# A scaled matmul with an addend on one core: tile 55 stored by GpSimd's queue in 32 pieces, and a last store of four tiles in place of eight

## The chip, the core and the metric

The kernel runs on one NeuronCore of one Trainium2 chip. The metric is the device time of one execution in microseconds (us), the median of three runs. Five engines work beside each other: TensorE (PE) multiplies, VectorE (DVE), ScalarE (ACT) and GpSimd (POOL) move and combine data, and SyncE (SP) issues transfers. Sixteen DMA queues move the data between HBM and the on-chip memory; the profile calls them the core's 16 DMA engines.

## What is computed

```python
def reference(x, weight, scale, add_value):
    # x: 16 x 512 x 1024, weight: 1024 x 768, add_value: 16 x 512 x 768, all float32; scale 0.1
    return (scale * np.matmul(x, weight) + add_value).astype(np.float32)
```

The 16 x 512 rows are taken as 8192 rows of one matrix.

## The kernel before

**Tiles.** The 8192 rows are 64 tiles of 128 rows. Sixteen neighbouring rows of HBM belong to one partition, so that tiles s to s+n-1 of one group are n consecutive rows in HBM for each partition. A transfer of n tiles is thus 128 runs, one for each partition: 4096 n bytes for `x`, 3072 n bytes for `add_value` and the output. Eight output tiles are 24,576 bytes in a partition, four are 12,288, one is 3,072.

**Buffers.** `xs` has 16 slots for tiles of `x`, `ao` has 32 slots which first hold the weights, then the addend and, after the sum is made in place, the output. `slot(t)` gives a tile's slot.

**Engines.** ACT and POOL cast `x` to bf16 and regroup it into `va` (`mover`, line 147, one half of the 32-partition blocks each). DVE transposes four-tile halves of `va` into `xt` (`turn`, line 162), PE multiplies (line 197), and DVE makes scale times product plus addend for two tiles at a time (`finish`, line 171). Each `finish` adds 2 to the semaphore `made`; its value `MADE` + t + 1 says that tiles up to t are done.

**SP's order.** `sync_engine` walks through the list `STREAM`: `w`, `x` and `a` are loads, `("o", s, n)` is the store of tiles s to s+n-1. SP waits for `made` ahead of each store. The first load of `x` (`FIRST`) stands ahead of the block and the last store (`LAST`, tiles 56 to 63, line 237) behind it. All other work stands in one block, `tc.tile_critical`, at whose exit SP collects a signal from every engine's sequencer, POOL's among them, before the store of line 237 is issued. At the very end SP waits for the last store to have landed (line 268).

**The end of the order.** The last transfers on SP are the loads of the addend for tiles 56 to 63, and the stores of tiles 32 to 47, 48 to 55 and 56 to 63. POOL has nothing to do once its last cast is done.

Of the kernel before, what the change touches and what calls it, by code (L numbers as in the profile page):

```python
# [8 lines left out]
P = 128  # L9
G = 8  # L10
R = 16
# [16 lines left out]
]  # L28
FIRST, LAST = (0, 8), (56, 8)


@with_exitstack
def kernel(
# [8 lines left out]
    nc = tc.nc  # L42
# [7 lines left out]
    _, N = weight.shape  # L50
    T = M // P
# [5 lines left out]
    out_v = out_f.rearrange("(g p t) n -> p g t n", p=P, t=R)  # L57
    w_v = weight.rearrange("(c p r) n -> p c (r n)", p=P, r=2)

    def rows(view, s, n):  # L60
        assert s // R == (s + n - 1) // R
        return view[:, s // R, s % R:s % R + n, :]
# [5 lines left out]
    ao = const.tile([P, A_SLOTS, N], fp32, name="ao")  # L68
# [6 lines left out]
    x_sem = [tc.alloc_semaphore(f"x{i}") for i in range(X_SLOTS // MOVE)]  # L75
    a_sem, a_late = (tc.alloc_semaphore(n) for n in ("a", "a_late"))
    o_sem = [tc.alloc_semaphore(f"o{i}") for i in range(2)]
    by_act, by_pool, pool_go, turned, casts, done, made = (
        tc.alloc_semaphore(name)
        for name in ("by_act", "by_pool", "pool_go", "turned", "casts", "done", "made"))  # L80
    TURNED = MOVE * VA_BUFS
    MADE = TURNED + 2 + MM_BUFS - 2

    def slot(t):
        return (t + G) % A_SLOTS

    def sync_engine(eng):
        loads, stores, known = [], [], {}

        def need(sem, value):  # L90
            if known.get(sem, 0) < value:
                eng.wait_ge(sem, value)
                known[sem] = value

        for op, s, n in STREAM:
            last = s + n - 1
            if op == "w":
                dst = ao[:, s:s + n, :].rearrange("p (c r) n -> p c (r n)", r=2)
                move, sem = eng.dma_start(dst, w_v[:, s // 2:(s + n) // 2, :]), w_sem[s // 4]
            elif op == "x":  # L100
                k = s % X_SLOTS
                if last >= X_SLOTS:
                    moved = 8 * (last + 1 - X_SLOTS) // MOVE
                    need(by_act, moved)
                    need(by_pool, moved)
                move = eng.dma_start(xs[:, k:k + n, :], rows(x_v, s, n))
                sem = x_sem[k // MOVE]
            elif op == "a":
                if loads and s % G == 0:
                    need(a_sem, 16 * len(loads))  # L110
                if slot(s) == 0:
                    need(casts, KJ)
                if s >= A_SLOTS:
                    i = next(j for j, (a, b) in enumerate(stores) if a <= s - A_SLOTS < a + b)
                    need(o_sem[i % 2], 16 * (i // 2 + 1))
                move = eng.dma_start(ao[:, slot(s):slot(s) + n, :], rows(add_v, s, n))
                if s % G:
                    sem = a_late
                else:
                    sem = a_sem  # L120
                    loads.append((s, n))
            else:
                i = len(stores)
                if i > 1:
                    need(o_sem[i % 2], 16 * (i // 2))
                need(made, MADE + last + 1)
                move = eng.dma_start(rows(out_v, s, n), ao[:, slot(s):slot(s) + n, :])
                sem = o_sem[i % 2]
                stores.append((s, n))
            move.then_inc(sem, 16)  # L130
            if op == "x" and n == 2 * MOVE:
                eng.sem_inc(x_sem[k // MOVE + 1], 16)

    def mover(eng, copy, parity, count, go=None):
        if go is None:
            eng.preload_act_table(mybir.ActivationFunctionType.Copy)  # L136
        with eng.Fori(16, 16 * (T // X_SLOTS) + 1, 16) as i:
            for q in range(X_SLOTS // MOVE):
                eng.wait_ge(x_sem[q], i)
                eng.wait_ge(turned, i + (4 * q - 12) if q < 3 else i)  # L140
                if go is not None:
                    eng.sem_inc(go, 1)
                k = MOVE * q
                src = xs[:, k:k + MOVE, :].rearrange("p i (c b k) -> p (i c) b k", b=4, k=64)
                for a in (parity, parity + 2):
                    for b in range(4):
                        copy(va[q % VA_BUFS][32 * b:32 * b + 32, :, a, :],  # L147
                             src[32 * a:32 * a + 32, :, b, :]).then_inc(count, 1)

    def vector_engine(eng):  # L150
        ao_g = ao.rearrange("p (g t) n -> p g t n", t=G)

        def cast_w(s, n):
            eng.wait_ge(w_sem[s // 4], 16)
            eng.tensor_copy(w_bf[:, s:s + n, :], ao[:, s:s + n, :]).then_inc(casts, n)  # L155

        def turn(move, half, moves=None):
            if half == 0:
                eng.wait_ge(by_act, moves)
                eng.wait_ge(by_pool, moves)  # L160
            q = 2 * half * KC
            eng.transpose(  # L162
                xt[:, 2 * half:2 * half + 2, :, :].rearrange("p i c m -> p (i c m)"),
                va[move % VA_BUFS][:, q:q + 2 * KC, :, :].bitcast(fp32).rearrange("p c a k -> p (c a k)"),
            ).then_inc(turned, 2)

        def finish(pair, at, products):
            eng.wait_ge(done, products)  # L168
            a = ao_g[:, at, 2 * pair:2 * pair + 2, :]
            q = 2 * (pair % 2)  # L170
            eng.scalar_tensor_tensor(  # L171
                a, mm[:, q:q + 2, 0:N], float(scale), a,
                op0=mybir.AluOpType.mult, op1=mybir.AluOpType.add).then_inc(made, 2)

        def group(i, at, last):
            eng.wait_ge(a_sem, i)
            for p in range(4):
                if p == 2 and not last:
                    eng.wait_ge(a_late, i)
                finish(p, at, i + (4 * p - 12) if p < 3 else i)  # L180
                if p < 2 or not last:
                    turn(1 if p < 2 else 0, p % 2, i + 8 if p == 2 else i)

        cast_w(0, 4)
        cast_w(4, 4)
        turn(0, 0, 8)
        turn(0, 1)
        with eng.Fori(16, 2 * T, 16) as i:
            group(i, bass.ds((i // 16) % (A_SLOTS // G), 1), False)
        eng.addr_align(HALF_BLOCK, offset=PAST)  # L190
        s = slot(T - G) // G
        group(2 * T, slice(s, s + 1), True)
# [12 lines left out]
    def tensor_engine(eng):  # L205
        eng.sem_inc(x_sem[1], 16)
        eng.sem_inc(turned, TURNED)
        eng.sem_inc(made, MADE)
        eng.sem_inc(a_late, 16 * (T // G - 2))
        eng.wait_ge(casts, KJ)  # L210
        with eng.Fori(TURNED + 2, TURNED + 2 + T, XT_TILES) as i:
            for q in range(XT_TILES):
                if q % 2 == 0:
                    eng.wait_ge(turned, i + q if q else i)
                    eng.wait_ge(made, i + q if q else i)
                for j in range(KJ):
                    x2 = xt[:, q, j // 2, :].bitcast(bf16).rearrange("p (m r) -> p r m", r=2)
                    m = product(eng, mm[:, q, :], x2[:, j % 2, :], w_bf[:, j, :], j)
                if q % 2:
                    m.then_inc(done, 4)  # L220


    s, n = FIRST
# [4 lines left out]
    with tc.tile_critical(no_gpsimd_drain=True):  # L228
        sync_engine(nc.sync)
        mover(nc.scalar, nc.scalar.copy, 0, by_act)  # L230
        nc.scalar.addr_align(HALF_BLOCK, offset=PAST)
        mover(nc.gpsimd, nc.gpsimd.tensor_copy, 1, by_pool, pool_go)
        nc.gpsimd.addr_align(HALF_BLOCK, offset=PAST)
        vector_engine(nc.vector)
        tensor_engine(nc.tensor)
    s, n = LAST
    nc.sync.dma_start(rows(out_v, s, n), ao[:, slot(s):slot(s) + n, :])


# [33 lines left out]
```

## Time and profile before

| what | value |
|---|---|
| median of 3 runs | 209.19 us (209.13 to 209.28) |
| span of the profiled execution | 207.5 us |
| what lies around the span, median less span | 1.7 us |
| PE busy | 168.4 us, 81% of the span |
| DVE, ACT, POOL busy | 97.8, 134.7, 135.4 us |
| moved by DMA | 87.06 MB, of which 25.17 MB are written to HBM |

The page of the profiled execution gives its span, the time from the first to the last instruction, and no time of its own beside it. The numbers of the trace below are times from the start of that span. In the views by windows the last two columns are the busy share of the 16 DMA queues and the rate; both count a packet, whole, in the window in which it starts. A packet is one run of bytes, or the 4 bytes that count up a semaphore when a queue has finished its part of a transfer.

### The profile page before, as it was taken

Reading aid. Unit: us, or ns where it says so; the run is one execution under the profiler, and the core shown is the slowest. Engines: PE = TensorE matmul, PEld = TensorE weight load, DVE = VectorE, ACT = ScalarE, POOL = GpSimd, SP = SyncE. Lnnn points to the kernel's source line nnn. Section 1 sums busy time; section 2 is a strip of 40 time slices with the busy share of each in tenths; the row PEclk is TensorE's granted clock in tenths of the full one; section 3 lists DMA queues with packets and bytes.
Section 4 is the critical chain, followed back from the end, with each engine's and each line's share of the span. In section 5 each row is a group of like instructions: output and inputs, shape, how many; then the busy total and the mean of one; then the engine's idle time right before and its main releaser. Section 6 shows DMA issues by size and latency. Waiting matters only on the chain.

```text
span 207.5 us, 2310 instructions
## 1 busy us (share of the span) xinstructions
PE 168.4 (81%) x1024; PEld 50.3 (24%) x512; DVE 97.8 (47%) x66; ACT 134.7 (65%) x129; POOL 135.4 (65%) x132
## 2 busy tenths in 40 slices
PE   0000099999999999999999999999999999999400
PEld 0000023333332222222233333333333333333100
DVE  0005525537555555555555554755555555553300
ACT  2059970799999796969696079999970999300000
POOL 0049994799999996969696079999990899400000
PEclk9999999999999999999999999999999999999955
DMA  7999999999999999999999999999999999999993
GB/s 291 417 381 469 403 466 404 455 455 404 404 467 442 411 398 486 393 441 407 445 436 423 423 436 455 411 445 412 441 414 422 437 445 455 460 417 388 412 441 171
DMA packets 4147, 87.06 MB, mean 420 GB/s; under 512 B 432, under 2 KB 432, under 8 KB 944
## 3 DMA queue, kind: packets, MB, share of 16 engines
q1 hardware_dynamic: 4144, 87.03, 98.1%
q14 instruction: 3, 0.02, 0.0%
HBM read 61.87 MB, written 25.17 MB: 419 GB/s over the span
## 4 chain that ended last, share of the span: by engine, by line
PE 81%; DMA 6%; ACT 5%; DVE 1%; issue 1%; DVEq 0%; ACTq 0%
PE mm L197 81%; DMA xs<-in_x_dram 6%; ACT va L147 5%; DVE ao L171 1%; DVE xt L162 1%; ACTq L140 0%; DVEq L160 0%; DVEq L168 0%
## 5 line engine op out<-in xcount | busy, mean ns | idle before, releaser
L197 PE MATMUL mm<-w_bf,xt 128*128 128x512 bf16 (+1 forms) x1024 | 168.4, 328 | 26.0 <-DVE xt L162 26.0
L147 POOL CAST va<-xs 32x1024 bf16<-32x1024 f32 x128 | 135.2, 1056 | 43.1 <-DMA xs<-in_x_dram 24.7
L147 ACT CAST va<-xs 32x1024 bf16<-32x1024 f32 x128 | 133.4, 1042 | 42.1 <-DMA xs<-in_x_dram 25.8
L171 DVE SCALAR_TENSOR_TENSOR ao<-mm,ao 128x1536 f32 (+1 forms) x32 | 56.3, 1758 | 76.5 <-PE mm L197 76.5
L195 PEld LDWEIGHTS <-xt 128*128 128x128 bf16 x512 | 50.3, 98 | 143.6 <-issue 117.6
L162 DVE STREAM_TRANSPOSE xt<-va 128x1024 f32<-128x1024 f32 x32 | 39.4, 1234 | 3.8 <-ACT va L147 2.1
L155 DVE CAST w_bf<-ao 128x3072 bf16<-128x3072 f32 x2 | 4.5, 2240 | 18.1 <-DMA ao<-in_weight_dram 18.1
L136 ACT ACT_TABLE_LOAD x1 | 1.3, 1283 | 1.3 <-SPq L228 1.3
L254 POOL MEMSET const-float32-0.0<- 128x1 f32 x1 | 0.1, 98 | 0.2 <-issue 0.2
L254 POOL MEMSET const-bfloat16-1.0<- 128x1 bf16 x1 | 0.1, 100 | 0.0
L254 POOL MEMSET const-float32-1.0<- 128x1 f32 x1 | 0.1, 98 | 0.0
L254 POOL MEMSET const-uint8-127<- 128x1 uint8 x1 | 0.1, 97 | 0.0
## 6 DMA issues: line engine op xcount, KB each, us to landing
xs<-in_x_dram SPq DMA_DIRECT2D x7, 4096.0 KB, 20.9
ao<-in_add_value_dram SPq DMA_DIRECT2D x7, 3072.0 KB, 17.0
out_dram<-ao SPq DMA_DIRECT2D x6, 3072.0 KB, 27.0
out_dram<-ao SPq DMA_DIRECT2D x1, 6144.0 KB, 35.4
xs<-in_x_dram SPq DMA_DIRECT2D x2, 2048.0 KB, 19.1
ao<-in_weight_dram SPq DMA_DIRECT2D x2, 1536.0 KB, 16.8
ao<-in_add_value_dram SPq DMA_DIRECT2D x2, 1536.0 KB, 14.9
```

Source lines behind the costliest of these rows:

```text
L136: eng.preload_act_table(mybir.ActivationFunctionType.Copy)
L147: copy(va[q % VA_BUFS][32 * b:32 * b + 32, :, a, :], src[32 * a:32 * a + 32, :, b, :]).then_inc(count, 1)
L155: eng.tensor_copy(w_bf[:, s:s + n, :], ao[:, s:s + n, :]).then_inc(casts, n)
L162: eng.transpose(xt[:, 2 * half:2 * half + 2, :, :].rearrange("p i c m -> p (i c m)"), va[move % VA_BUFS][:, q:q + 2 * KC, :, :].bitcast(fp ...
L171: eng.scalar_tensor_tensor(a, mm[:, q:q + 2, 0:N], float(scale), a, op0=mybir.AluOpType.mult, op1=mybir.AluOpType.add).then_inc(made, 2)
L195: eng.ldweights(x_j, tile_position=(0, 0))
L197: m = eng.add_instruction(mybir.InstMatmult(start_tensor_calc=(j == 0), stop_tensor_calc=(j == KJ - 1), tile_size=(P, P), tile_position=(0 ...
L254: nc = _bacc.Bacc("TRN2", target_bir_lowering=False, num_devices=1)
```

## The change

- The store of tiles 48 to 55 becomes one of tiles 48 to 54 (`("o", 48, 7)`).
- Tiles 56 to 59 get a store of their own on SP behind it, once they are made, with a semaphore `end_sem` that nobody waits for. The last store has tiles 60 to 63.
- Tile 55 is stored by GpSimd's queue (`aside`), behind its last cast and once tile 55 is made. It is cut into 16 sets of eight partitions, each set four partitions apart (q, q+4, ... q+28). Each set is two transfers: one of the last 32 columns of either half of the row (16 runs of 128 bytes, 2 KB), and one of the other 352 columns of either half (16 runs of 1408 bytes, 22 KB). Together they are 32 transfers, 2 KB and 22 KB in turn. They stand inside the block.
- Behind the last store SP waits, in a second small block, until all 32 have landed (`few_sem`).

```diff
-    ("a", 52, 4), ("x", 60, 4), ("a", 56, 8), ("o", 32, 16), ("o", 48, 8),
+    ("a", 52, 4), ("x", 60, 4), ("a", 56, 8), ("o", 32, 16), ("o", 48, 7),
+    ("o", 56, 4),
 ]
-FIRST, LAST = (0, 8), (56, 8)
+FIRST, LAST = (0, 8), (60, 4)
+ASIDE, FEW, STEP, FILL = 55, 8, 4, 32
...
+    few_sem, end_sem = (tc.alloc_semaphore(name) for name in ("few", "end"))
...
+            elif last == T - LAST[1] - 1:
+                need(made, MADE + last + 1)
+                move = eng.dma_start(rows(out_v, s, n), ao[:, slot(s):slot(s) + n, :])
+                sem = end_sem
...
+    def aside(eng):
+        eng.wait_ge(made, MADE + ASIDE + 1)
+        to = out_v[:, ASIDE // R, ASIDE % R, :].rearrange("p (h n) -> p h n", h=2)
+        at = ao[:, slot(ASIDE), :].rearrange("p (h n) -> p h n", h=2)
+        for p in range(0, P, FEW * STEP):
+            for q in range(p, p + STEP):
+                part = slice(q, q + (FEW - 1) * STEP + 1, STEP)
+                for n in (slice(N // 2 - FILL, N // 2), slice(0, N // 2 - FILL)):
+                    eng.dma_start(to[part, :, n], at[part, :, n]).then_inc(few_sem, 16)
...
         nc.gpsimd.addr_align(HALF_BLOCK, offset=PAST)
+        aside(nc.gpsimd)
...
     s, n = LAST
     nc.sync.dma_start(rows(out_v, s, n), ao[:, slot(s):slot(s) + n, :])
+    with tc.tile_critical(no_gpsimd_drain=True):
+        nc.sync.wait_ge(few_sem, 16 * 2 * P // FEW)
```

No other engine's instructions change; the loads, casts, transposes and products keep their order.

## The prediction

> **What bounds the kernel now.** I read the page's slices first, then the DMA queues, the chain, and the end of the run by windows.
>
> ```profile
> PE   0000099999999999999999999999999999999400
> DMA  7999999999999999999999999999999999999993
> q1 hardware_dynamic: 4144, 87.03, 98.1%
> PE 81%; DMA 6%; ACT 5%; DVE 1%; issue 1%; DVEq 0%; ACTq 0%
> ```
>
> Two things are full at once. PE works without a gap from the sixth slice on, and the chain puts 81% of the span on it; but the chain view stops at the last instruction on an engine and leaves out the transfer behind it. The DMA queues are busy for 98.1% of the span. PE sets when the last tiles are made; the queues set when everything has landed.
>
> ```profile
> 26.01 168.37 PE mm L197 x1024
> 194.48 1.76 DVE L171 SCALAR_TENSOR_TENSOR ao<-mm,ao 128x1536 f32<-128x1536 f32 x1 [3.44 <-PE mm L197]
> 196.53 0.33 SPq L237 DMA_DIRECT2D out_dram<-ao  x1
> DMA to landing us min/median/max: 10.1/10.1/10.1
> SPq L268 <- DMA out_dram<-ao: 9.7, 1, 9.7
> ```
>
> The last tile is made at 194.48 + 1.76 = 196.24, the last store is issued at 196.53 and has landed 10.1 us later, at 206.6; SP waits 9.7 us for it. Behind that lie 0.9 us to the span's end at 207.5 and 1.7 us more to the median of 209.19. So the change can act on the 10.1 us alone, or on the time at which they begin.
>
> What fills them is seen in windows (the last two columns are the queues' share and GB/s, by the packets that start in each):
>
> ```profile
> 178.75:196.50 17.75, 15.62 (x97) 4.59 (x47) 9.33 (x6) 0.00 (x0) 0.00 (x0) 1.00 0.99 425
> 196.90:197.30 0.40, 0.00 (x0) 0.00 (x0) 0.00 (x0) 0.00 (x0) 0.00 (x0) 0.53 0.29 123
> 197.35:198.25 0.90, 0.00 (x0) 0.00 (x0) 0.00 (x0) 0.00 (x0) 0.00 (x0) 0.50 1.02 437
> 203.70:204.35 0.65, 0.00 (x0) 0.00 (x0) 0.00 (x0) 0.00 (x0) 0.00 (x0) 0.50 1.41 605
> 204.35:205.15 0.80, 0.00 (x0) 0.00 (x0) 0.00 (x0) 0.00 (x0) 0.00 (x0) 0.50 0.01 0
> 205.20:206.20 1.00, 0.00 (x0) 0.00 (x0) 0.00 (x0) 0.00 (x0) 0.00 (x0) 0.50 0.06 25
> ```
>
> (1) When the last store is issued the queues still hold older stores: 0.99 up to 196.50. (2) From 196.90 to 197.30 the share falls to 0.29: queues that have run dry wait for the last store's first packets, which start about 0.85 us after the issue, at 197.35 or so. The loss is (0.99 - 0.29) x 0.40 = 0.28 us, a mean over the 16 queues. (3) Between 203.70 and 204.35, 605 GB/s x 0.65 us = 393 KB start, 16 packets of 24,576 bytes, each 1.41 x 16 x 0.65 / 16 = 0.917 us long; up to 205.15 no data follows; after 205.20 exactly one packet more starts (25 GB/s x 1.00 us). So fifteen queues are through between 203.70 + 0.917 = 204.6 and 204.35 + 0.917 = 205.3, and one late queue, a packet behind, at 205.2 + 0.92 = 206.1. That one queue sets the landing. It had no dry moment to lose: it began its last eight packets 8 x 0.917 = 7.3 us earlier, at 198.8, when the store had long been there.
>
> **The change part by part.** *SP's stores.* Tile 55 leaves the store of 48 to 55: 8 partitions x 3,072 = 24,576 bytes less on each queue, -0.92 us. Eight tiles in two stores of four are eight packets and a semaphore write more on each. The 4-byte writes between 204.35 and 205.15 take 0.01 x 16 x 0.80 = 0.13 us for the fifteen queues that end there, 9 ns each; I take that as the fixed cost of a packet, so 9 x 9 ns = +0.08. The store of 56 to 59 comes in time: tiles 58 and 59 are made by the third `finish` from the end.
>
> ```profile
> 184.08 1.76 DVE L171 SCALAR_TENSOR_TENSOR ao<-mm,ao 128x1536 f32<-128x1536 f32 x1 [2.26 <-PE mm L197]
> 170.05 8.70 POOL L147 CAST va<-xs 32x1024 bf16<-32x1024 f32 x8
> L228 POOLq NOP  x1: 13/13/13, 175.9 to 175.9; - x1
> 175.50 0.34 SPq L127 DMA_DIRECT2D out_dram<-ao  x1
> ```
>
> At 185.84 it is issued, while the queues are full to 196.5 and beyond, so the dry moment of (2) is closed for the queues that had it: -0.28 us in the mean, nothing for the late one. What would undo this cover is a last store issued so late that the four tiles ahead of it (half of 7.3, 3.7 us) are through.
>
> *Tile 55 on GpSimd's queue.* No row shows a transfer issued there, nor how eight partitions are dealt over sixteen queues. Each transfer has 16 runs. If they fall on eight queues, two on each, and the next transfer takes the other eight, the 2 KB pieces always meet the same half and the 22 KB pieces the other. On a queue of the small half, 32 runs of 128 bytes are 32 x (5 + 9) ns = +0.45, and up to 32 semaphore writes +0.29: with -0.92 and +0.08 that is **-0.10 us**. On a queue of the large half, 32 runs of 1,408 bytes are 45,056 bytes, 1.68 us, and 0.29 for the packets and 0.29 for the semaphores: with -0.92 and +0.08, **+1.42 us**. Bounds for the short runs: bytes alone (0.15 in place of 0.45, 1.68 in place of 1.97, no semaphores) gives -0.69 and +0.84; from above, a short run could cost twice its packet, +0.35 and +1.9. I take 9 ns, the only measured packet of few bytes. If instead all 32 fall on the same eight queues, these get 49,152 bytes, 1.83 + 0.58 + 0.29 - 0.84 = +1.86; if they spread evenly, the bytes come back to every queue and only pieces and semaphores are added, about +0.6.
>
> The Trainium skill (DMA: Bandwidth & Descriptors, "Why a DMA increments its semaphore by 16 and not by 1") says that a software-generated transfer with fewer than sixteen outer steps goes to that many consecutive queues, from a cursor that moves round. By that rule it is the halves in turn; no row of this trace tests it, and it doesn't say in which half the late queue lies.
>
> *The time of issuing.* POOL's last cast ends at 170.05 + 8.70 = 178.75, and only then can the 32 start (tile 55 is made by 175.50, when SP issues the store that holds it). SP issues behind the block's exit, which waits for POOL's sequencer. That sequencer runs ahead: its signal, the NOP of line 228, came at 175.9, while casts ran to 178.75, some 2.8 us, which is two to three instructions at 8.70 / 8 = 1.09 us. So it signals when the 29th of the 32 starts. The nearest rows for an issue are SP's:
>
> ```profile
> 146.20 0.82 SPq L116 DMA_DIRECT2D ao<-in_add_value_dram  x1
> 156.18 0.33 SPq L116 DMA_DIRECT2D ao<-in_add_value_dram  x1
> ```
>
> At 0.33 us each POOL is through at 178.75 + 10.6 = 189.3; at 0.82, at 205.0, with the signal at 178.75 + 28 x 0.82 = 201.7. GpSimd has to write sixteen runs of a transfer rather than hand it over, and SP's long issues are those with a crowd behind them; I take the middle, 0.58, which ends at 197.3 with the signal at 195.0, ahead of the last tile at 196.24: no cost.
>
> The Trainium skill (the same page, "Latency and other measured facts") gives about 1 us to the first byte on the software path, for the descriptors' making. If that were the pace of a row of issues, the sum would be the first rival's at 1 us.
>
> *SP's end.* The second block adds a round of SP's own events behind the landing. The first block's exit took 196.53 - 196.24 = 0.29 with another engine in it; +0.15 is my estimate, 0 to 0.29 the bounds.
>
> *Sum.* With the late queue in the small half: it ends at 206.12 - 0.10 = 206.0. A queue of the large half, without its dry moment: 204.6 to 205.3, less 0.28, plus 1.42 = 205.7 to 206.4. The last data ends about 206.1, as before; the landing is where it was; +0.15 for the end. Span 207.65, and with the same 1.7 us around it **209.3 us**, 0.1 above the median.
>
> **The rivals.** *POOL's issues hold back the last store* (slower). The mechanism is the exit of the block: if an issue takes t, the last store is issued no earlier than 178.75 + 28 t + 0.25, its data starts 0.85 later and takes 3.7 us on each queue, and 0.5 passes to the landing. This overtakes 206.6 where 28 t exceeds 22.6, so from t = 0.81 us. At 0.82, SP's longest, it costs nothing to speak of; at 1.0 us the landing is 212.0, so 209.19 + 5.4 + 0.15 = 214.8; at 0.9, 212.0. For it: sixteen runs are written by a processor, for two addresses each, and SP's hardware already needs up to 0.82. Against it: SP's usual 0.33 leaves a factor of two and a half.
>
> *The late queue lies in the loaded half* (or among eight that take everything). It then ends at 206.12 + 1.42 = 207.54, and the time is 209.19 + 1.42 + 0.15 = 210.8 (up to 211.2). Nothing in the profile names the queue; the dealing of the first transfer decides. An even spread, 209.19 + 0.6 + 0.15 = 209.9, belongs here: the change then doesn't single out a half.
>
> *The short runs cost their bytes alone, and the late queue is relieved*: 206.12 - 0.69 = 205.4, the large half 204.3 to 205.0 + 0.84 = 205.2 to 205.9. The landing comes 0.3 to 0.7 earlier; with no cost at SP's end the time is 208.6. For it: packets follow one another without a gap (share 0.99). Against it: the 9 ns of a semaphore write.
>
> **How the numbers follow.** Forecast 209.3, own range 208.8 to 209.7: 0.37. POOL's issues 0.26, the loaded half or the even spread 0.19, the gain 0.18. A measurement of this kernel can tell 0.2% from no change, 0.42 us: faster is below 208.77, slower above 209.61. Faster takes the gain and a sliver of the forecast, 0.22; slower takes both rivals above and some of the forecast's upper end, 0.48; 0.30 is left for no change. The range runs from 208.4 (the gain's end, with a little for the bound of -0.69) to 212.0 (POOL at 0.9 us an issue); outside lie POOL above that, 0.13, and some 0.05 below.
>
> **What would show it.** POOL's rows of the new line: the distance of two issues is t, and the last store's issue against 196.53 shows whether the exit held it. The windows at the end: one lone queue after the others means the late one was not relieved; eight together, that the large pieces set the end. Between 196.9 and 197.3 the share should be near 0.99. The landing of the last store, and the time between it and the span's end (0.9 before), give SP's end. The forecast is wrong if the last store is issued after 201, or if the landing is more than 0.4 us away from 206.6.

## The result, and the profile after

| | before | after |
|---|---|---|
| median of four runs on one chip | 209.24 us | 214.81 us (213.95 to 214.87) |
| ratio, after to before | | 1.0255 (95%: 1.0242 to 1.0267) |
| profiled execution: its own time, its span | not given, 207.5 us | 214.87 us, 213.1 us |

The changed kernel is 5.6 us slower, outside the predicted range. Its median is the number that the first rival gave for POOL at 1.0 us an issue, and yet that rival didn't happen, as the next rows show. They are from the timeline and from the views by source line of the changed kernel: start and length in us, or the shortest, median and longest of a group in ns, with the first and the last start.

```profile
181.20 17.89 POOL L165 DMA_DIRECT2D out_dram<-ao  x32 [2.21 <-issue]
195.07 1.76 DVE L188 SCALAR_TENSOR_TENSOR ao<-mm,ao 128x1536 f32<-128x1536 f32 x1 [3.44 <-PE mm L214]
197.11 0.33 SPq L255 DMA_DIRECT2D out_dram<-ao  x1
```

```profile
L165 POOL DMA_DIRECT2D out_dram<-ao x32: 557/557/691, 181.2 to 198.5; - x32
L245 POOLq NOP  x1: 13/13/13, 196.9 to 196.9; - x1
DMA to landing us min/median/max: 12.3/12.3/12.3
```

An issue takes 0.557 us. POOL's signal at the block's exit comes at 196.9, the last tile is made at 195.07 + 1.76 = 196.83, and the last store is issued at 197.11, 0.28 behind the tile as before (196.53 - 196.24 = 0.29). So the exit held nothing back. But the store lands 12.3 us after its issue and not 10.1: at 209.4.

Behind the landing more follows. These are rows of the last source line, that of the program's end:

```profile
L288 SPq EVENT_SEMAPHORE  x6: 17/22/1471, 197.6 to 213.0; - x6
L288 SPq DRAIN  x3: 7/7/7, 211.3 to 212.5; - x3
L288 POOLq DRAIN  x3: 39/118/15256, 197.0 to 212.8; - x3
L288 POOLq EVENT_SEMAPHORE  x4: 17/17/17, 212.3 to 213.0; - x4
```

SP has its store at 209.4 and then waits another 1.471 us for the last count-ups of GpSimd's transfers, to 210.9. It is through with the second block and its own drains at 211.4. POOL meanwhile stands in one drain that started at 197.0 and lasts 15.256 us, to 212.2. Only then do the engines' last events run, from 212.3, to the span's end at 213.1. The difference of the two spans, from these rows and those of the prediction:

| step | before | after | adds |
|---|---|---|---|
| last store issued | 196.53 | 197.11 | 0.6 |
| issue to landing | 10.1 | 12.3 | 2.2 |
| landing to the last count-up | none | 1.5 | 1.5 |
| to the end of SP's second block, 211.4 | none | 0.5 | 0.5 |
| to the end of POOL's drain, 212.2 | none | 0.9 | 0.9 |
| the last events, to the span's end | 0.9 | 0.8 | -0.1 |
| sum | | | 5.6 |

In 197.11 one delay is hidden that is not the change's: PE's full clock began at 30.94 us in this execution and at 29.67 in the one before, and DVE's last sum lies 0.59 later (195.07 against 194.48). Such shifts stand in most kernels of this study: their first product starts between 25.9 and 26.2 us, their full clock between 28.7 and 31.9. The landing does not follow them: in e7_block below the last tile is made at 196.70, and the landing is at 206.5. The Trainium skill (TensorE: Matmul & The Clock Gate, "Part 1: The HAM clock gate (the "warmup" mystery)") calls the window of the gate free-running and its start variable from run to run; the traces agree, with the spread just given.

The landing's 2.8 us are seen in the windows. First before, then after; the last two columns are the queues' share and GB/s:

```profile
195.00:200.00 5.00, 0.00 (x0) 0.00 (x0) 1.24 (x1) 0.00 (x0) 0.00 (x0) 0.69 0.95 408
200.00:203.00 3.00, 0.00 (x0) 0.00 (x0) 0.00 (x0) 0.00 (x0) 0.00 (x0) 0.50 1.09 467
203.00:206.00 3.00, 0.00 (x0) 0.00 (x0) 0.00 (x0) 0.00 (x0) 0.00 (x0) 0.50 0.46 197
206.00:209.00 3.00, 0.00 (x0) 0.00 (x0) 0.00 (x0) 0.00 (x0) 0.00 (x0) 0.50 0.00 0
```

```profile
195.00:200.00 5.00, 0.00 (x0) 0.00 (x0) 1.76 (x1) 0.00 (x0) 4.09 (x8) 0.82 1.01 372
200.00:203.00 3.00, 0.00 (x0) 0.00 (x0) 0.00 (x0) 0.00 (x0) 0.00 (x0) 0.50 1.16 327
203.00:206.00 3.00, 0.00 (x0) 0.00 (x0) 0.00 (x0) 0.00 (x0) 0.00 (x0) 0.50 0.83 292
206.00:209.00 3.00, 0.00 (x0) 0.00 (x0) 0.00 (x0) 0.00 (x0) 0.00 (x0) 0.50 0.43 169
```

Between 195 and 203 the queues are busier than before and move less: 372 x 5 + 327 x 3 = 2,841 KB against 408 x 5 + 467 x 3 = 3,441 KB. The missing 600 KB are made up after 203. GpSimd's packets themselves are cheap:

```profile
q1 hardware_dynamic: 4288, 86.64, 96.2%
q0 software_dynamic: 1024, 0.40, 0.7%
```

(queue, packets, MB, share of 16 engines): 0.7% of 213.1 us is 1.5 us on a queue. The rest has to be that SP's own packets last longer. In the trace's packet records, SP's packets from 193 us on last 30.8 us more in all than the median of earlier packets of their size (between two sizes, by interpolation), 30.8 / 16 = 1.9 us on each queue. In e1_split below, without GpSimd's transfers, that sum is under 0.1.

### The profile page after: what moved, and what is told of

It is laid out like the page before. It is cut to its first block, busy times and chain, and to the rows that moved or that the text cites. A ratio compares the mean times of both kernels' runs of the same rounds, so it can differ in the third digit from the quotient of the medians.

```text
span 213.1 us, 2335 instructions
## 1 busy us (share of the span) xinstructions
PE 168.2 (79%) x1008; PEld 50.5 (24%) x512; DVE 97.8 (46%) x66; ACT 134.7 (63%) x129; POOL 153.4 (72%) x164
## 3 DMA queue, kind: packets, MB, share of 16 engines
q0 software_dynamic: 1024, 0.40, 0.7%
## 4 chain that ended last, share of the span: by engine, by line
PE 30%; DMA 24%; ACT 16%; POOL 15%; issue 6%; DVE 1%; POOLq 1%; DVEq 0%; ACTq 0%
PE mm L214 30%; DMA xs<-in_x_dram 24%; ACT va L154 16%; POOL out_dram L165 8%; POOL va L154 7%; DVE xt L179 1%; POOLq L288 0%; POOLq L250 0%; DVE ao L188 0%; DVEq L205 0%; ACTq L144 0%; ACTq L147 0%; DVEq L188 0%; DVEq L177 0%; DVEq L185 0%
## 5 line engine op out<-in xcount | busy, mean ns | idle before, releaser
L214 PE MATMUL mm<-w_bf,xt 128*128 128x256 bf16 (+1 forms) x1008 | 168.2, 328 | 26.8 <-DVE xt L179 25.9
L165 POOL DMA_DIRECT2D out_dram<-ao x32 | 17.9, 562 | 2.2 <-issue 2.2
## 6 DMA issues: line engine op xcount, KB each, us to landing
xs<-in_x_dram SPq DMA_DIRECT2D x7, 4096.0 KB, 20.9
```

Of the source, the lines that this page charges most:

```text
L165: eng.dma_start(to[part, :, n], at[part, :, n]).then_inc(few_sem, 16)
L214: m = eng.add_instruction(mybir.InstMatmult(start_tensor_calc=(j == 0), stop_tensor_calc=(j == KJ - 1), tile_size=(P, P), tile_position=(0 ...
```

## The experiments

The expectations name the explanations by letters. A: the number of GpSimd's transfers sets the loss, through their count-ups and the drain; D is the same with the reason that a queue serves GpSimd's packets in turn with SP's. B: anything on GpSimd's queue is dear, whatever its number. C: runs of 128 bytes are slow. E: each transfer costs a fixed time, whenever it is served. Beside these stands the prediction's second rival, that the late queue lies in the half with the large pieces. Unless said otherwise the diffs are against the changed kernel. "Before" is the median of the kernel before on the same chip.

**e1_split: SP's stores alone.** The last store is of four tiles; tile 55 is back on SP, there is no second block.

```diff
-    ... ("o", 32, 16), ("o", 48, 7),
+    ... ("o", 32, 16), ("o", 48, 8),
-        aside(nc.gpsimd)
-    with tc.tile_critical(no_gpsimd_drain=True):
-        nc.sync.wait_ge(few_sem, 16 * 2 * P // FEW)
```

> The changed kernel with tile 55 back in SP's store of tiles 48 to 55, no transfer on GpSimd's queue and no second block: the last store of eight tiles is two of four and nothing else. All theories of the loss on GpSimd's side: the 5.6 us are gone, 209.2 (208.9 to 209.4), since the late queue has no dry moment to lose. The share between 196.9 and 197.3 rises from 0.29 to about 0.99. Rival (the split store itself costs a part): 209.8 or more.

Measured 209.34 us, before 209.18, ratio 1.0006 (0.9997 to 1.0015): no change. In the dry moment of the prediction, its first window below, the share is 0.86 in place of 0.29, and still the store lands at 196.49 + 10.2 = 206.7:

```profile
196.90:197.30 0.40, 0.00 (x0) 0.00 (x0) 0.00 (x0) 0.00 (x0) 0.00 (x0) 0.50 0.86 369
```

So the dry moment is closed, and that is worth nothing. All of the loss lies with GpSimd's transfers and the second block.

**e2_one: tile 55 in one GpSimd transfer of 128 partitions.**

```diff
+        eng.dma_start(rows(out_v, ASIDE, 1), ao[:, slot(ASIDE):slot(ASIDE) + 1, :]).then_inc(few_sem, 16)
```

> Tile 55 still on GpSimd's queue, as one transfer of 128 partitions in place of 32 pieces; second block kept. Theory A (each transfer's count-ups of its semaphore hold up the queues, so the price goes with the number of transfers): the last store lands within 0.5 us of before, and GpSimd's drain is over before SP's end; 209.5 (209.2 to 209.9). Rival B (anything issued on GpSimd's queue makes the drain at the end and the queues slow, whatever its number): 211 or more, the drain still ends over 1 us behind the landing.

Measured 209.65 us, ratio 1.0023 (1.0014 to 1.0032). The store lands 9.8 us after its issue at 197.13, at 207.0, and the span ends at 208.3, 1.3 behind it, in place of 0.9. The same bytes on GpSimd's queue thus cost next to nothing, as long as they are one transfer. That is A's number, and B falls.

**e3_sixteen: sixteen transfers of eight whole rows.** The two pieces of a set become one transfer.

```diff
-                for n in (slice(N // 2 - FILL, N // 2), slice(0, N // 2 - FILL)):
+                for n in (slice(0, N // 2),):
```

> Sixteen transfers of eight whole rows, without the 2 KB pieces: half the transfers, the same bytes, no run under 512 bytes. Theory A (price by the transfer): about half of the 5.6 us stays, 212 (211.2 to 212.8). Rival C (the 128-byte runs are what is slow): nearly all goes, 209.6 to 210.2. Rival B (the queue as such): 213.5 or more.

Measured 211.42 us, ratio 1.0106 (1.0091 to 1.0122). The issues take 0.518 us each, the store lands at 197.19 + 10.7 = 207.9, and the drain lasts to 187.5 + 21.3 = 208.8.

```profile
L288 POOLq DRAIN  x3: 34/118/21320, 187.5 to 209.3; - x3
```

```profile
190.00:195.00 5.00, 5.00 (x32) 1.37 (x14) 1.70 (x1) 0.00 (x0) 0.00 (x0) 1.00 1.01 428
195.00:200.00 5.00, 0.04 (x1) 0.00 (x0) 1.76 (x1) 0.00 (x0) 0.00 (x0) 0.82 0.98 414
```

At 428 and 414 GB/s nothing is missing while sixteen transfers are served. The loss of 2.2 us is a landing 1.3 us later than before (206.6), and some 0.4 each of second block and drain. It lies in A's range; C and B, which expected nearly nothing or nearly all of the loss, were off.

**e4_act: the same 32 transfers on ScalarE's queue.** The call of `aside` moves from `nc.gpsimd` to `nc.scalar`.

> The same 32 transfers, issued by ACT (idle since its last cast) in place of GpSimd. Theory A (price by the transfer, whoever issues): 212 to 214, spread on eight fixed queues. Rival B (software-made transfers and GpSimd's drain are the price): 209.5 to 211, with no drain behind the landing. Rival C (the 128-byte runs): 213 or more, as the runs are the same.

Measured 214.72 us, ratio 1.0269 (1.0254 to 1.0285): the same time by another way. From the timeline, the view by source line and the waits:

```profile
176.24 29.42 ACTq L165 DMA_DIRECT2D out_dram<-ao  x32
206.33 0.33 SPq L255 DMA_DIRECT2D out_dram<-ao  x1
```

```profile
L165 ACTq DMA_DIRECT2D out_dram<-ao x32: 685/706/5592, 176.2 to 205.0; - x32
SPq L245 <- ACTq L245: 9.1, 1, 9.1
```

Here the first rival's mechanism is real, which none of the three expectations had. ACT's longest issue takes 5.59 us, the other 31 about 0.77 each (23.8 us for all of them); ACT is through at 205.7, and the block's exit holds the last store until 206.33. It then lands in 5.0 us, at 211.4, and POOL has nothing to drain. So this run says nothing for or against A, B or C. In the changed kernel POOL's 0.557 us kept that away.

**e5_halves: equal pieces.** `FILL` is 192: 32 transfers as before, all runs 768 bytes.

> The changed kernel with the rows cut in the middle (FILL 192): still 32 transfers of eight partitions on GpSimd's queue, but every run is 768 bytes. Theory D (a queue serves GpSimd's packets in turn with SP's, so the price goes with their number, and 64 for each queue are too many for the SP packets that are left): 214.3 to 215.3, as with 128 and 1408 bytes. Rival C (the 128-byte runs are the price): 211 to 212.5.

Measured 214.81 us, ratio 1.0272 (1.0256 to 1.0288): the time of the changed kernel to a hundredth. The landing comes earlier, at 197.10 + 11.1 = 208.2, SP's wait for the count-ups is longer, 2.632 us, and the drain ends at 212.2 again (196.72 + 15.447). The time is in D's range. So runs of 128 bytes are not the cause, and C falls.

**e6_mixed: sixteen small transfers and one large.** The sixteen 2 KB pieces, then all the 22 KB pieces as one transfer of 128 partitions.

```diff
+                n = slice(N // 2 - FILL, N // 2)
+                eng.dma_start(to[part, :, n], at[part, :, n]).then_inc(few_sem, 16)
+        n = slice(0, N // 2 - FILL)
+        eng.dma_start(to[:, :, n], at[:, :, n]).then_inc(few_sem, 16)
```

> The sixteen 2 KB pieces as they were, and all the rest of tile 55 as one transfer of 128 partitions: 17 transfers, all 128-byte runs still there. Theory D (number of transfers): as with sixteen whole rows, 211.0 to 212.0. Rival C (the 128-byte runs): 213.5 or more.

Measured 210.49 us, ratio 1.0066 (1.005 to 1.0081), below what was expected. The landing, at 196.92 + 9.4 = 206.3, is not delayed at all; the time lost is SP's wait of 0.912 us for the count-ups, the second block and the drain. So 17 transfers cost less than e3's 16, and their number alone doesn't give the landing.

**e7_block: the second block alone**, added to e1_split.

```diff
+    with tc.tile_critical(no_gpsimd_drain=True):
+        nc.sync.wait_ge(end_sem, 16)
```

> Only the split last store, and a second block behind it that waits for the store of tiles 56 to 59, long landed: the price of the block by itself. From the changed kernel's SP events (0.5 us from the landing to the end's barrier, 0.12 before): 0.38 us, so 209.6 to 209.8. If the block is free: 209.2 to 209.4.

Measured 209.66 us, ratio 1.0026 (1.0015 to 1.0036). From landing to the span's end it takes 1.31 us, in e1_split 0.93: the block costs 0.38, and e2_one's small loss is mostly this.

**e8_relief: the late queue spared.** In e1_split, tile 31 is stored as 120 and 8 partitions. This was to leave the last queue a packet less.

```diff
-    ... ("o", 24, 8), ...
+    ... ("o", 24, 7), ("r", 31, 1), ...
+                for a, z in ((0, 120), (120, P)):
+                    eng.dma_start(rows(out_v, s, n)[a:z], ao[a:z, slot(s):slot(s) + n, :]).then_inc(few_sem, 16)
```

> The split last store, and tile 31 taken out of the store of tiles 24 to 31 and stored by SP in two transfers, partitions 0 to 119 and 120 to 127: should the first be dealt over fifteen queues, the sixteenth carries 24,576 bytes less. If that is the late queue, the landing comes 0.8 us earlier, 208.4 (208.2 to 208.7). If the late queue is another, or the dealing is not by fifteen, 209.2 to 209.8.

Measured 210.09 us, ratio 1.0039 (1.0026 to 1.0053): a miss, outside both ranges. One queue does end 0.57 us ahead of the others (204.32 against 204.88), but it isn't the late one, which comes 1.3 us behind them; the landing is at 197.0 + 10.5 = 207.5. Which queue is late, and whether it is the same in each execution, stays open.

**e9_turns and e10_cut: more turns.** The trace's packet records of the changed kernel, counted by window (16 queues together), show whose turn it was:

```
us          185-190  190-195  195-200  200-203  203-206  206-210
SP's            44      104      137       78       70       53
GpSimd's        41      103      139      501       71      169
```

While both have work, a queue takes one packet of each in turn. SP's are up to 24,576 bytes long and last 0.9 us, GpSimd has 1,024 / 16 = 64 packets for each queue, and by 200 us only 283 of 1,024 have been served, though all 32 transfers are issued by 199.1 (181.20 + 17.89). So the count-ups come late. If that is all of it, many short packets on SP give GpSimd enough turns. e9 cuts SP's stores from tile 32 on into transfers of one or two tiles; e10 is the same cut in e1_split, as its control.

```diff
+    def cut(eng, s, n, c):
+        for b in range(s, s + n, c):
+            eng.dma_start(rows(out_v, b, c), ao[:, slot(b):slot(b) + c, :]).then_inc(end_sem, 16)
...
+                c = n if s < 32 else 2 if n == 16 else 1
+                cut(eng, s, n - c, c)
+                b = s + n - c
+                move = eng.dma_start(rows(out_v, b, c), ao[:, slot(b):slot(b) + c, :])
```

> The changed kernel with SP's stores from tile 32 on cut along the tiles: eight transfers of two tiles, seven of one, four of one, and the last store of four whole. A queue then has 64 + 56 + 32 short SP packets from 157 us on in place of 8 + 8 + 8. Theory D (one packet in turn with SP's): GpSimd's 64 packets for each queue find their turns early, no crowd of them at 200 to 203 us and at the end; the last count-up comes before 208 and the time falls well below the changed kernel's, 210 to 212. Rival E (each transfer costs its queues a fixed time, whenever it is served): 214.5 or more, as there are more transfers.

> The control to the run before: the same cut stores on SP, the split last store, nothing on GpSimd's queue, no second block. Both theories: the split store's 209.3 and some 0.1 us for each eight packets and each count-up more, 209.4 to 210.5. What the run before has beyond this one is the price of tile 55 on GpSimd's queue where turns are plenty.

e9 took 213.0 us, ratio 1.0178 (1.0161 to 1.0195), e10 209.94, ratio 1.0033 (1.0021 to 1.0044). In e9 the last count-up is there at 203.4, six microseconds ahead of the landing, and the drain is over as well (196.1 + 8.7 = 204.8):

```profile
L296 POOLq DRAIN  x3: 39/118/8732, 196.1 to 210.9; - x3
```

So the tail behind the landing comes from the lack of turns: with turns it is gone but for 0.46 us (from the landing to the span's end 1.77, in e7_block 1.31; 0.42 of the rest lies between two of SP's own events), and 1.8 us are won against the changed kernel. But e9 is still 3.1 us slower than its control, and lands 2.2 us later (209.4 against 207.2). Of D's two numbers the count-up's came (before 208) and the time's did not (210 to 212); E's 214.5 or more did not come either.

The records say more exactly how a lack of turns makes the tail. A count-up has two times: the record of its 4-byte write on a queue, and its arrival at the semaphore. In e9 the last write's record ends at 203.07 and the last arrival is at 203.43. In the changed kernel the last of GpSimd's writes ends at 208.52, ahead of SP's last one (208.98), and still the last count-up arrives only at 210.87, 2.36 us behind. So no count-up waits for a turn at the very end. The lack of turns gathers them into crowds, and the arrivals of a crowd lag behind its writes. The windows, first e9 and then e10:

```profile
190.00:200.00 10.00, 4.78 (x30) 1.32 (x14) 3.20 (x2) 0.00 (x0) 8.16 (x15) 0.88 1.02 364
200.00:203.00 3.00, 0.00 (x0) 0.00 (x0) 0.00 (x0) 0.00 (x0) 0.00 (x0) 0.50 1.03 383
```

```profile
190.00:200.00 10.00, 5.47 (x34) 1.56 (x16) 3.52 (x2) 0.00 (x0) 0.00 (x0) 0.96 1.03 413
200.00:203.00 3.00, 0.00 (x0) 0.00 (x0) 0.00 (x0) 0.00 (x0) 0.00 (x0) 0.50 1.08 443
```

At the same share e9 moves 364 GB/s for 413. The 49 GB/s over ten microseconds and 60 over three are 670 KB, at 413 GB/s 1.6 of the 2.2 us. While POOL's 32 transfers are being served, a queue needs longer for the same bytes, and turns don't cure it.

**e11_mid: 24 transfers.** Every other set is one transfer, the rest stay cut in two.

```diff
+                whole = (slice(0, N // 2),)
+                for n in whole if q % 2 else (slice(N // 2 - FILL, N // 2), slice(0, N // 2 - FILL)):
```

> Between sixteen and thirty-two: every other set of eight rows whole, the others in the two pieces, 24 transfers, 48 packets for each queue. Theory D: not half way, since the packets beyond the turns are what costs; 212 to 213.5, with a crowd at 200 to 203 between the two. Rival E (fixed price for each transfer): half way between 211.4 and 214.8, 213.1.

Measured 212.37 us, ratio 1.0148 (1.0131 to 1.0165): in D's range, and below E's half way of 213.1. The landing is at 197.14 + 9.9 = 207.0, SP waits 1.682 us more for the count-ups, and the drain lasts to 192.8 + 16.9 = 209.7.

```profile
L289 SPq EVENT_SEMAPHORE  x6: 17/22/1682, 197.6 to 210.5; - x6
L289 POOLq DRAIN  x3: 34/118/16916, 192.8 to 210.3; - x3
```

**e12_swap: the 22 KB piece first.** By the prediction's dealing the large pieces then fall on the other half of the queues.

```diff
-                for n in (slice(N // 2 - FILL, N // 2), slice(0, N // 2 - FILL)):
+                for n in (slice(0, N // 2 - FILL), slice(N // 2 - FILL, N // 2)):
```

> The changed kernel with the order of the two pieces swapped, the 22 KB piece first: if the pieces go to the two halves in turn, the other half of the queues now takes the large ones. If the dealing decides (the prediction's second rival) and the late queue was spared in the changed kernel: the last store lands about 1.5 us later than there, 216 to 216.8. If the halves don't matter beside the price of the count-ups and the drain: 214.5 to 215.2.

Measured 214.56 us, ratio 1.0257 (1.024 to 1.0274). The landing does move, to 196.98 + 10.4 = 207.4, two microseconds ahead of the changed kernel's, and the time hardly does:

```profile
L288 SPq EVENT_SEMAPHORE  x6: 17/22/3182, 197.4 to 212.7; - x6
L288 POOLq DRAIN  x3: 34/118/14962, 197.0 to 212.5; - x3
```

SP's wait for the count-ups is now 3.182 us, and the drain ends at 211.9. What the landing gives, the wait takes. With 32 transfers it isn't the last store that sets the end, but the last count-up and the drain behind it; the second rival, which rests on the late queue, falls as the cause of the time.

**The runs side by side**, in us of each profiled span (the last count-up is its arrival in the trace's semaphore records):

| kernel | transfers | landing | last count-up | span's end | end less count-up |
|---|---|---|---|---|---|
| e3_sixteen | 16 | 207.9 | 208.08 | 209.61 | 1.53 |
| e6_mixed | 17 | 206.4 | 207.27 | 208.85 | 1.58 |
| e11_mid | 24 | 207.0 | 208.72 | 210.58 | 1.86 |
| after | 32 | 209.4 | 210.87 | 213.06 | 2.19 |
| e5_halves | 32 | 208.2 | 210.80 | 212.99 | 2.19 |
| e12_swap | 32 | 207.4 | 210.55 | 212.74 | 2.19 |

The last column goes with the number of transfers alone: (2.19 - 1.53) / 16 = 0.041 us for each. The landing of the last store does not order these rows, the last count-up does. None of the twelve kernels was faster than the kernel before; e1_split is its equal.

## Why the prediction was wrong, point by point

- **The step that failed** is the sum's last: "The last data ends about 206.1, as before; the landing is where it was; +0.15 for the end." Two things were left out. Behind the landing the span ends 3.65 us later (213.06 - 209.41), where 0.9 + 0.15 were put: the last count-ups (1.5), the second block (0.5), POOL's drain (0.9) and the last events (0.8). The prediction counted the semaphore writes as work on a queue, and never as something that the end waits for. And the landing is 2.8 us late, though the prediction's reason for "as before" was that a queue's work is the sum of its packets.
- **The price of the packets was right, as a price.** The halves were to carry 0.45 + 0.29 and 1.97 + 0.29 us, in the mean 1.50; GpSimd's packets took 25.6 us over 16 queues in the trace, 1.60 each. "9 ns" is the median of its 4-byte writes. What the sum lacked is that SP's packets on the same queues grew, by 1.9 us on each.
- **Halves in turn** was right: in the records the data go as 128 packets of 256 and 128 of 2,816 bytes, two runs in one packet. The records don't name the queue; but wherever two data packets can be followed on one queue without doubt, a small one is followed by a small one (21 times) and a large one by a large one (21 times), never otherwise. That is the rule quoted in the prediction, and the trace agrees with it. As e12_swap shows it doesn't decide the time.
- **POOL's issues**: 0.58 was taken, 0.557 came. That the exit holds nothing was right, but by a hair, and its margin was worked out too large. The signal was put at 195.0 and came at 196.9, because POOL stood 2.21 us idle between its last cast and the first issue. Had the last tile been made a microsecond earlier, the exit would have held the store: in e12_swap the signal comes at 196.9 too, the last tile is made at 195.74, and the store is issued at 196.98. The 1 us to the first byte that the prediction took from the Trainium skill (DMA: Bandwidth & Descriptors, "Latency and other measured facts") was not the pace of a row of issues; the rows show 0.557.
- **SP's split** was right: no gain, since the late queue had no dry moment to lose, and no loss (e1_split). The test that the prediction named, a share near 0.99 between 196.9 and 197.3, read 0.82 in the changed kernel and 0.86 in e1_split.
- **SP's end**: +0.15, with 0.29 as the upper bound; e7_block measured 0.38. Why it is dearer than the exit that had served as the model, no run shows.
- **The rivals.** The first came to the right number for the wrong kernel: its mechanism was absent in the changed kernel and was shown with the transfers on ACT (e4_act). The second and the gain did not happen: one of the queues that finish last in the changed kernel can be followed through the records from 206.53 to 208.86, and the data piece that it serves is a small one, so this queue is of the half that the prediction had relieved. No rival had the end wait for GpSimd's last count-ups.

**What stays open.** Why SP's packets last longer while many of GpSimd's transfers are served. Packets in flight stay 16, one for each queue; small runs (e5_halves) and a lack of turns (e9_turns, 12.0 us of queue time in all) don't explain it; with 16 transfers it is 1.7 us, with 24 it is 11.0, and with 32 it is 20.9 (e12_swap) to 30.8 (the changed kernel).

And the crowd of 501 GpSimd packets to 78 of SP's from 200 to 203 us. The records show where it stands, though not why. Wherever it can be followed, a run of GpSimd's packets begins behind the count-up with which one of SP's stores ends (6 times: here tiles 56 to 59, after 206 us the last store), and behind SP's data one packet of GpSimd's comes and then SP's again (259 times). Until the last store's first packets come, SP's packets hold 8 to 11 of the sixteen queues (201.0 to 202.5), in e1_split all sixteen. So a dry moment, which the split store was to close, opened again some four us after the last store's issue at 197.11; what held its first packets back, no run shows. Some of these packets then last very long, up to 2.28 us in place of 0.46. Neither this nor the late arrivals were tried further.

## What to carry to other kernels

A transfer on GpSimd's queue is paid three times: when it is issued, in its count-ups, which wait their turn behind the other queue's packets and arrive late when they come in a crowd, and in POOL's drain at the program's end. Near the end of this kernel, fewer and larger transfers were better than a clever division of bytes: the same tile cost 0.5 us in one transfer, 2.2 in sixteen and 5.6 in 32, the second block included. And when a forecast's sum ends at a landing, list everything that the program's last events wait for, and price each from the landing on.

## What the runs showed of the hardware

- POOL's drain goes on after the last count-up by 0.70 us at 16 transfers, 1.03 at 24 and 1.36 to 1.37 at 32: about 0.043 us for each transfer. Where SP's packets were short (e9_turns) it was 1.36 too.
- Every GpSimd transfer writes sixteen count-ups, though its data are eight packets: 512 writes of 4 bytes for 32 transfers. The Trainium skill (DMA: Bandwidth & Descriptors, "Why a DMA increments its semaphore by 16 and not by 1") says the same of the software path: all sixteen engines post one. A small transfer thus brings 16 count-ups, 8 writes of 8 bytes and 8 data packets in this kernel.
- The same page ("Queues, rings and completion order") lets a queue change over between rows of work packet by packet, with typically nine to seventeen descriptors to a packet. The records show one of SP's and one of GpSimd's in turn, 104 to 103 and 137 to 139, where a record of SP's is a run of 12,288 or 21,504 bytes, so here a turn of SP's was a single run. From 185 us on, wherever it can be followed, one of SP's was followed by one of GpSimd's 326 times and by another of SP's 4 times.
- The last count-ups of the changed kernel arrive 0.19 us apart (210.13, 210.32, 210.50, 210.69, 210.87), twenty times the 9 ns that the records give for such a write; the last arrives at least 2.36 us after its record, in e9_turns 0.36.
- An issue of eight partitions took 0.518 us with eight runs and 0.557 with sixteen on POOL, and about 0.77 us on ACT.
